# An attention kernel's last two pairs: one store moved to GpSimd's queue, some blocks and copies moved between VectorE and ScalarE

## The chip, the core and the metric

The kernel runs on one core of a Trainium2 chip. The metric is the device time of one execution in microseconds; a profiled execution also gives a span, from its first to its last recorded instruction, and a trace of all instructions and DMA packets.

## What is computed

The reference is linear attention with the feature map relu(x) + 1. For each of 8 x 12 heads, with 512 positions of 64 features (all fp32):

```python
    Q_feat = np.maximum(0, Q) + 1
    K_feat = np.maximum(0, K) + 1
    KV = np.einsum('bhkd,bhkv->bhdv', K_feat, V)
    K_sum = np.sum(K_feat, axis=2)
    numerator = np.einsum('bhqd,bhdv->bhqv', Q_feat, KV)
    denominator = np.einsum('bhqd,bhd->bhq', Q_feat, K_sum)
    return (numerator / (denominator[:, :, :, None] + 1e-10)).astype(np.float32)
```

## The kernel before

The 96 heads are worked on in 12 groups (`g`, 0 to 11) of 8 heads, two groups to a pair (`s`, 0 to 5; NG is 12). Each input of a pair is 2 MB in memory and is loaded by one software DMA from GpSimd's queue, which turns it into bf16 (1 MB in SBUF). The result of a group is 1 MB of fp32.

What each step does, with its line in the profile and its engine:

- `k_features` and `q_features` (L172, VectorE): the feature map, max(x + 1, 1). K's is four instructions of 64x1024 in the pairs 0, 4 and 5 (the list `WIDE`), two of 128x1024 elsewhere; Q's is two of 128x1024 for a group.
- `v_blocks` (L193 on VectorE, L195 on ScalarE): V times each of four 0/1 masks, into `v_all`, so that one product keeps four heads apart. Each of the four masks is one instruction of 128x2048. A cut of 2 gives a mask's whole block to VectorE, a cut of 0 to ScalarE.
- `keys_values` (L219 in the wide pairs, L229 elsewhere, TensorE): K features by V blocks, summed in PSUM (`kva_ps`). It is issued in quarters, with other work in between. `keys_values_copies` (L244) brings the sums to SBUF as bf16 (`kva_all`), in four copies for each pair.
- `transposes` (L257, TensorE) and `transpose_copies` (L262, ScalarE): the Q features turned, through PSUM, into `qt`.
- `out_matmuls` (L275, TensorE) into `o_ps`, and `norms` (L291 and L292, VectorE): the reciprocal of the denominators and the product with the numerators, into `o_sb`. A group has four cells, and `norms` runs once for each.
- `store` (L156 on GpSimd's queue, L161 to L169 on SyncE's): a group's 1 MB to memory. Groups 0 to 9 go by one software DMA each. Group 10 goes by one hardware DMA of SyncE, and group 11 by five smaller ones (512, 256, 61.5, 2.5 and 192 KB).

The order is written out by hand: each engine runs its instructions in the order in which the program issues them. `iteration(s)`, with a = 2s and b = 2s + 1, computes the outputs of the pair before (`output(a - 2)`, `output(a - 1)`) while it makes the key-value sums of its own pair. `output` calls what it is given in `between` after its first and second norms; that is where quarters of `keys_values`, the transposes and, in the last pair alone, the K features of group 11 are put. V blocks for ScalarE are issued at the iteration's top (group b) and before the keys-values copies (the next pair's group a).

Pairs 0 and 1 are started before the loop. Loads are issued two pairs ahead, and the first stores only after iteration 3, behind the last load. So all stores stand in GpSimd's queue behind all loads. After the loop come the outputs of groups 10 and 11 and the stores of both.

Of the kernel before, what the change touches and what calls it, by code (L numbers as in the profile page):

```python
# [19 lines left out]
def kernel(  # L20
# [15 lines left out]
    nc = tc.nc  # L36
# [8 lines left out]
    NP = 4  # L45
    NG = NPAIR // NP
    D1 = D + 1
    W = 2 * D1
    DV = D + 4
# [48 lines left out]
    outs = {}  # L98
# [53 lines left out]
    def store(g):  # L152
        s = g // 2
        o_to = o_dram[:, 2 * NP * s : 2 * NP * s + 2 * NP]
        if g < NG - 2:
            nc.gpsimd.dma_start(  # L156
                out=o_to[:, g % 2 : 2 * NP : 2], in_=outs[s][:, g % 2 : 2 * NP : 2], single_packet=True
            )
            return
        if g == NG - 2:  # L160
            nc.sync.dma_start(out=o_to[:, 0 : 2 * NP : 2], in_=outs[s][:, 0 : 2 * NP : 2])  # L161
            return
        o_sb = outs[s]
        nc.sync.dma_start(out=o_to[:, 1 : 2 * NP : NP], in_=o_sb[:, 1 : 2 * NP : NP])
        nc.sync.dma_start(out=o_to[:, 3], in_=o_sb[:, 3])
        cut = C - 2
        for ps in (slice(0, 123), slice(123, P)):
            nc.sync.dma_start(out=o_to[ps, 7, cut:], in_=o_sb[ps, 7, cut:])
        nc.sync.dma_start(out=o_to[:, 7, 0:cut], in_=o_sb[:, 7, 0:cut])  # L169
# [6 lines left out]
    def k_features(g):  # L176
        k_raw = raw.pop(("k", g))
        kf = kf_of(g)
        for n in range(2):
            if g // 2 in WIDE:  # L180
                for h in range(2):
                    ps = slice(64 * h, 64 * h + 64)
                    feature(kf[ps, :, n, h], k_raw[ps, n])
            else:
                feature(kf[:, :, n], k_raw[:, n])

    def v_blocks(g, engine):
        v_raw = raw["v", g]
        for b in range(4):
            block = v_all[:, g % 2, :, :, b, 0:D]  # L190
            cut = 2 if b < 2 and g < NG - 1 else 0
            if engine == "dve" and cut > 0:
                nc.vector.tensor_scalar_mul(block[:, 0:cut], v_raw[:, 0:cut], mask[:, b : b + 1])  # L193
            if engine == "act" and cut < 2:
                nc.scalar.mul(out=block[:, cut:], in_=v_raw[:, cut:], mul=mask[:, b : b + 1])  # L195

    def q_features(g):
        q_raw = raw.pop(("q", g))
        qf = qf_pool.tile([P, R, C // 4, 2, D, 2], BF16, name="qf")
        for n in range(2):  # L200
            feature(
                qf[:, :, :, n].rearrange("p r c d x -> p r c x d"),
                q_raw[n].rearrange("p r (c x) d -> p r c x d", x=2),
            )
        qfs[g] = qf

    def keys_values(g, lo=0, hi=C2):
        kf = kf_of(g)
        if g % 2 == 0 and lo == 0:
            kva_ps[g // 2] = [psum_kva.tile([P, BANK], FP32, name="kva_ps") for _ in range(2)]  # L210
        halves = kva_ps[g // 2]
        for c in range(lo, hi):
            for n in range(2):
                if g < 2:
                    eight, first, last_c = g, (c, n) == (0, 0), (c, n) == (C2 - 1, 1)
                else:
                    eight, first, last_c = n, g % 2 == 0 and c == 0, g % 2 == 1 and c == C2 - 1
                if g // 2 in WIDE:
                    nc.tensor.matmul(  # L219
                        halves[eight][:, 0 : 4 * DV],  # L220
                        lhsT=kf[:, c, n],
                        rhs=v_all[:, g % 2, n, c],
                        start=first,
                        stop=last_c,
                    )
                    continue
                for h in range(2):
                    ps = slice(64 * h, 64 * h + 64)
                    nc.tensor.matmul(  # L229
                        halves[h][64 * eight : 64 * eight + 64, 0 : 4 * DV],  # L230
                        lhsT=kf[ps, c, n],
                        rhs=v_all[ps, g % 2, n, c],
                        start=first,
                        stop=last_c,
                    )

    def keys_values_copies(s):
        halves = kva_ps[s]
        for h in range(2):
            kva = kva_diag[(2 * s + h) % NV]  # L240
            for n in range(2):
                ps = slice(64 * n, 64 * n + 64)
                tile_, at = (n, slice(64 * h, 64 * h + 64)) if s in WIDE else (h, ps)
                nc.scalar.copy(  # L244
                    out=kva[ps, :, n, :],
                    in_=halves[tile_][at, 0 : 4 * DV].rearrange("p (b x) -> p b x", b=4)[:, :, 0:D1],
                )

    def transposes(g):

        qf = qfs.pop(g).rearrange("p r c n d x -> p r c (n d x)").bitcast(FP32)
        if g % 2 == 0:
            qts[g // 2] = mid_pool.tile([P, C // 2, P, R, 2], BF16, name="qt")
        qt_ps[g] = [psum_qt.tile([P, R, P], FP32, name="qt_ps") for _ in range(2)]
        for half in range(2):
            for r in range(R):
                nc.tensor.transpose(qt_ps[g][half][:, r], qf[:, r, half], identity)  # L257

    def transpose_copies(g):
        to = qts[g // 2].rearrange("p c q r x -> p c (q r x)").bitcast(FP32)  # L260
        for half, t in enumerate(qt_ps.pop(g)):
            nc.scalar.copy(  # L262
                out=to[:, g % 2 * 2 + half].rearrange("p (q r) -> p q r", r=R),
                in_=t.rearrange("p r q -> p q r"),
            )
# [35 lines left out]
    def output(g, between=()):  # L301

        cells = [(g, h, i) for h in range(2) for i in range(2)]
        for k in range(4):
            if k >= 2:
                norms(*cells[k - 2])
                if k - 2 < len(between):
                    between[k - 2]()
            out_matmuls(*cells[k])
        norms(*cells[2])  # L310
        norms(*cells[3])

    def iteration(s):


        a, b = 2 * s, 2 * s + 1
        end = b == NG - 1
        quarter = C2 // 4

        def turned(g):  # L320
            transposes(g)
            transpose_copies(g)

        def first_half():
            turned(a)
            if not end:
                turned(b)
            keys_values(b, 0, quarter)

        def second_half():  # L330
            if end:
                turned(b)
            keys_values(b, quarter, 2 * quarter)

        def second_quarter():
            if end:
                k_features(b)
            keys_values(a, quarter, 2 * quarter)

        v_blocks(b, "act")  # L340
        output(a - 2, (lambda: keys_values(a, 0, quarter), second_quarter))
        keys_values(a, 2 * quarter, C2)
        q_features(a)
        q_features(b)
        if not end:
            k_features(b)
            v_blocks(b, "dve")
        output(a - 1, (first_half, second_half))
        keys_values(b, 2 * quarter, C2)
        if not end:  # L350
            v_blocks(a + 2, "act")
        keys_values_copies(s)
        if not end:
            k_features(a + 2)
            v_blocks(a + 2, "dve")
# [6 lines left out]
    with tc.manual_schedule():  # L362
# [7 lines left out]
        for t in kf_all:  # L370
# [3 lines left out]
            out=mask,  # L374
            in_=identity.rearrange("p (h b x) -> p b h x", h=2, b=4),
# [3 lines left out]
        for i in range(2):  # L379
# [3 lines left out]
                out=t[:, :, :, D], in_=mask[:, None, :].to_broadcast([P, 2 * C2, 4])  # L383
# [14 lines left out]
        keys_values(1)  # L398
        load_pair(2)
        keys_values_copies(0)  # L400
        blocks(2)
        for s in range(1, NG // 2):
            iteration(s)
            if s + 2 < NG // 2:
                load_pair(s + 2)
            for g in range(2 * s - 2, 2 * s) if s > 3 else range(2 * s) if s == 3 else ():
                store(g)
        output(NG - 2)
        output(NG - 1)
        for g in range(NG - 2, NG):  # L410
            store(g)
# [30 lines left out]
```

## Time and profile before

| | |
|---|---|
| Median of 3 runs | 125.42 us (125.40 to 125.49) |
| Profiled execution | 125.89 us, with a span of 124.1 us |
| VectorE busy | 91.3 us (74%) |
| TensorE busy | 77.2 us (62%) |
| ScalarE busy | 72.7 us (59%) |
| GpSimd busy | 26.4 us (21%) |
| DMA, software queue | 28.84 MB, 94.3% of 16 engines' span |
| DMA, hardware queue | 3.15 MB, 7.1% |
| HBM | 37.75 MB read, 12.58 MB written |
| Mean granted TensorE clock | 0.885 |

How to read the profile: times are microseconds from the start of the span. PE is TensorE, PEld its weight loads, DVE VectorE, ACT ScalarE, POOL GpSimd and SP SyncE; a q behind a name is that engine's queue. In a timeline a row is: start, time from its start to its end, engine, line, operation, output<-input with shapes, number of instructions, and in brackets the idle time before it and what ended it. In a table of stretches a row has the busy time of each engine with its count, the granted clock, the mean busy share of the 16 DMA engines and the GB/s that they moved (counted in the bytes written). A DMA lands when its semaphore has been raised; each of the engines that carry it raises it by a part when its own part is through, so that the packet records and the semaphore show when each engine was done.

### The profile page before, as it was taken

The numbers are of one execution on the slowest core, as the hardware profiler recorded it, in microseconds if no ns is written. First come the engines' busy times: TensorE is split into PE (matmuls) and PEld (weight loads), VectorE is DVE, ScalarE is ACT, GpSimd is POOL, SyncE is SP. The second block draws the span as 40 slices with busy tenths as digits, with TensorE's granted clock in tenths as the row PEclk, the third lists the DMA queues.
The fourth block names the chain that finished last, engine by engine and source line by source line (L and its number), as shares of the span: only waits on it lengthen the run. The fifth ranks groups of instructions, "written<-read, shape, count | busy, mean of one in ns | idle before, by whom it ended". The sixth has DMA issues, their size and how long they took to land.

```text
span 124.1 us, 2515 instructions
## 1 busy us (share of the span) xinstructions
PE 77.2 (62%) x1056; PEld 55.4 (45%) x1056; DVE 91.3 (74%) x187; ACT 72.7 (59%) x75; POOL 26.4 (21%) x52
## 2 busy tenths in 40 slices
PE   0000089992398768767699751999497797974500
PEld 0000057771266545645466541567256575762300
DVE  5789772009159999999979989659949999629920
ACT  0005939719982999499964999104943999331000
POOL 6990000600000330006000591210302008020000
PEclk9999999999559999999959996579869999999755
DMA  4999999999999999999999999999999999999993
GB/s 100 323 215 211 213 218 216 211 211 214 217 214 218 215 213 211 218 214 213 215 216 214 213 216 215 216 211 214 214 331 421 421 411 417 417 413 415 392 391 121
DMA packets 8900, 32.15 MB, mean 259 GB/s; under 512 B 568, under 2 KB 824, under 8 KB 8760
## 3 DMA queue, kind: packets, MB, share of 16 engines
q0 software_dynamic: 7520, 28.84, 94.3%
q1 hardware_dynamic: 1368, 3.15, 7.1%
q8 instruction: 8, 0.13, 0.4%
q14 instruction: 4, 0.03, 0.1%
HBM read 37.75 MB, written 12.58 MB: 406 GB/s over the span
## 4 chain that ended last, share of the span: by engine, by line
DVE 36%; PE 25%; DMA 20%; ACT 10%; issue 3%; POOL 1%; ACTq 0%; POOLq 0%
PE kva_ps L219 16%; DVE o_sb L292 13%; DMA k_raw<-in_K_dram 13%; DVE qf L172 7%; DMA v_raw<-in_V_dram 7%; ACT v_all L195 6%; DVE kf_all L172 6%; DVE v_all L193 6%; PE o_ps L275 4%; PE qt_ps L257 3%; DVE recip L291 3%; ACT qt L262 2%; PE kva_ps L229 2%; DVE o_sb L172 1%; ACT L195 1%
## 5 line engine op out<-in xcount | busy, mean ns | idle before, releaser
L195 ACT ACTIVATE v_all<-v_raw,mask 128x2048 bf16<-128x2048 bf16 x26 | 50.4, 1994 | 2.3 <-DMA v_raw<-in_V_dram 2.1
L219 PE MATMUL kva_ps<-v_all,kf_all 128*128 128x272 bf16 x192 | 30.0, 318 | 21.3 <-ACT v_all L195 15.8
L292 DVE TENSOR_TENSOR o_sb<-o_ps,recip 128x512 f32<-128x512 f32 x48 | 33.2, 692 | 1.6
L219 PEld LDWEIGHTS <-kf_all 128*128 128x128 bf16 x192 | 20.2, 109 | 28.1 <-DVE v_all L193 16.0
L275 PE MATMUL o_ps<-kva_all,qt 128*64 128x130 bf16 x384 | 20.2, 241 | 9.0 <-ACT kva_all L244 5.3
L262 ACT COPY qt<-qt_ps 128x512 f32<-128x512 f32 x24 | 12.9, 588 | 17.2 <-PE qt_ps L257 17.0
L275 PEld LDWEIGHTS <-qt 128*64 128x64 bf16 x384 | 13.8, 118 | 18.5 <-issue 9.2
L229 PE MATMUL kva_ps<-v_all,o_sb 64*64 64x272 bf16 x384 | 17.2, 316 | 7.0 <-ACT v_all L195 4.1
L291 DVE RECIPROCAL recip<-o_ps 128x8 f32<-128x8 f32 x48 | 9.7, 201 | 12.3 <-PE o_ps L275 12.3
L193 DVE TENSOR_SCALAR v_all<-v_raw,mask 128x2048 bf16<-128x2048 bf16 x22 | 15.6, 752 | 0.9 <-DMA v_raw<-in_V_dram 0.9
L156 POOL DMA_DIRECT2D out_dram<-o_sb x10 | 9.7, 980 | 29.2 <-DVE o_sb L292 21.9
L229 PEld LDWEIGHTS <-o_sb 64*64 64x64 bf16 x384 | 11.3, 120 | 9.9 <-issue 6.4
L257 PE MATMUL qt_ps<-identity,qf 128*128 128x128 f32 x96 | 13.3, 281 | 3.0 <-DVE qf L172 1.6
L172 DVE TENSOR_SCALAR qf<-q_raw 128x1024 bf16<-128x1024 bf16 x22 | 14.8, 751 | 0.4 <-DMA q_raw<-in_Q_dram 0.4
L129 POOL DMA_DIRECT2D v_raw<-in_V_dram x5 | 3.7, 731 | 54.0 <-ACT qt L262 41.1
L244 ACT CAST kva_all<-kva_ps 64x260 bf16<-64x260 f32 x24 | 8.9, 372 | 9.3 <-PE kva_ps L219 8.9
L172 DVE TENSOR_SCALAR kf_all<-k_raw 64x1024 bf16<-64x1024 bf16 x24 | 11.6, 484 | 1.6 <-DMA k_raw<-in_K_dram 1.3
L257 PEld LDWEIGHTS qt_ps<-identity,qf 128*128 128x128 f32 x96 | 10.2, 140 | 5.4 <-DVE qf L172 2.6
L172 DVE TENSOR_SCALAR o_sb<-k_raw 128x1024 bf16<-128x1024 bf16 x12 | 4.5, 422 | 8.4 <-DMA k_raw<-in_K_dram 8.4
L195 ACT ACT_TABLE_LOAD x1 | 1.3, 1283 | 10.6 <-DMA v_raw<-in_V_dram 10.6
L91 DVE MEMSET kf_all<- 64x1024 f32 x4 | 3.6, 912 | 1.8 <-PEq L426 1.0
L142 POOL DMA_DIRECT2D q_raw<-in_Q_dram x5 | 3.7, 733 | 0.0
(15 smaller groups left out, 14.0 us busy)
## 6 DMA issues: line engine op xcount, KB each, us to landing
out_dram<-o_sb POOLq DMA_DIRECT2D x10, 1024.0 KB, 23.9
v_raw<-in_V_dram POOLq DMA_DIRECT2D x5, 1024.0 KB, 13.0
k_raw<-in_K_dram POOLq DMA_DIRECT2D x5, 1024.0 KB, 17.2
q_raw<-in_Q_dram POOLq DMA_DIRECT2D x5, 1024.0 KB, 21.3
o_sb<-in_Q_dram SPq DMA_DIRECT2D x1, 1024.0 KB, 4.9
k_raw<-in_K_dram POOLq DMA_DIRECT2D x2, 512.0 KB, 9.6
v_raw<-in_V_dram POOLq DMA_DIRECT2D x2, 512.0 KB, 11.5
out_dram<-o_sb SPq DMA_DIRECT2D x1, 1024.0 KB, 5.0
```

What stands on the lines that cost most here:

```text
L156: nc.gpsimd.dma_start(out=o_to[:, g % 2 : 2 * NP : 2], in_=outs[s][:, g % 2 : 2 * NP : 2], single_packet=True)
L172: nc.vector.tensor_scalar(out=dst, in0=src, scalar1=1.0, scalar2=1.0, op0=ALU.add, op1=ALU.max)
L193: nc.vector.tensor_scalar_mul(block[:, 0:cut], v_raw[:, 0:cut], mask[:, b : b + 1])
L195: nc.scalar.mul(out=block[:, cut:], in_=v_raw[:, cut:], mul=mask[:, b : b + 1])
L219: nc.tensor.matmul(halves[eight][:, 0 : 4 * DV], lhsT=kf[:, c, n], rhs=v_all[:, g % 2, n, c], start=first, stop=last_c,)
L229: nc.tensor.matmul(halves[h][64 * eight : 64 * eight + 64, 0 : 4 * DV], lhsT=kf[ps, c, n], rhs=v_all[ps, g % 2, n, c], start=first, stop=l ...
L244: nc.scalar.copy(out=kva[ps, :, n, :], in_=halves[tile_][at, 0 : 4 * DV].rearrange("p (b x) -> p b x", b=4)[:, :, 0:D1],)
L257: nc.tensor.transpose(qt_ps[g][half][:, r], qf[:, r, half], identity)
L262: nc.scalar.copy(out=to[:, g % 2 * 2 + half].rearrange("p (q r) -> p q r", r=R), in_=t.rearrange("p r q -> p q r"),)
L275: nc.tensor.matmul(o_ps[64 * j : 64 * j + 64, c // 2 % 2, (c % 2) * W : (c % 2) * W + W], lhsT=qt[:, c // 2, q : q + 16, :, c % 2], rhs=kv ...
L291: nc.vector.reciprocal(out=recip, in_=cells[:, :, :, :, D:D1])
L292: nc.vector.tensor_tensor(out=outs[g // 2][:, 2 * h + g % 2 : 2 * NP : NP, 4 * i : 4 * i + 4].rearrange("p n (b c) d -> p b c n d", b=2), ...
```

## The change

Three things change, all in the last pairs.

1. The store of group 10 goes by one software DMA from GpSimd's queue, in the form that groups 0 to 9 have, in place of one hardware DMA of SyncE.
2. In pair 4 the odd group (9) gets the order that pair 5's odd group (11) has: ScalarE makes all four of its V blocks, where VectorE made two, and its K features are issued after the second norm of the outputs of group 6 (in `second_quarter`), where they came after the Q features of groups 8 and 9.
3. In the last pair (5) two of the four keys-values copies are made by VectorE, those with h equal to n.

```diff
     def store(g):
...
-        if g < NG - 2:
+        if g < NG - 1:
             nc.gpsimd.dma_start(
                 out=o_to[:, g % 2 : 2 * NP : 2], in_=outs[s][:, g % 2 : 2 * NP : 2], single_packet=True
             )
-            return
-        if g == NG - 2:
-            nc.sync.dma_start(out=o_to[:, 0 : 2 * NP : 2], in_=outs[s][:, 0 : 2 * NP : 2])
             return
...
-            cut = 2 if b < 2 and g < NG - 1 else 0
+            cut = 2 if b < 2 and g not in (NG - 3, NG - 1) else 0
...
-                nc.scalar.copy(
-                    out=kva[ps, :, n, :],
-                    in_=halves[tile_][at, 0 : 4 * DV].rearrange("p (b x) -> p b x", b=4)[:, :, 0:D1],
-                )
+                from_ = halves[tile_][at, 0 : 4 * DV].rearrange("p (b x) -> p b x", b=4)[:, :, 0:D1]
+                if s == NG // 2 - 1 and h == n:
+                    nc.vector.tensor_copy(out=kva[ps, :, n, :], in_=from_)
+                else:
+                    nc.scalar.copy(out=kva[ps, :, n, :], in_=from_)
...
+        late = b >= NG - 3
...
         def second_quarter():
-            if end:
+            if late:
                 k_features(b)
             keys_values(a, quarter, 2 * quarter)
...
-        if not end:
+        if not late:
             k_features(b)
             v_blocks(b, "dve")
```

## The prediction

> **What bounds the kernel now.** I read the page first: is an engine or the DMA full, and until when?
>
> ```profile
> DMA  4999999999999999999999999999999999999993
> ...
> q0 software_dynamic: 7520, 28.84, 94.3%
> q1 hardware_dynamic: 1368, 3.15, 7.1%
> ```
>
> The 16 DMA engines are full from 3 to 121 us; no compute engine is (VectorE 74%). The chain of waits ends in VectorE's norms, but a chain follows one releaser at a time and can't show that the transfers behind it are late anyway. So next the tail: SyncE's issues, and the DMA in half microseconds (last columns: granted clock, DMA share, GB/s).
>
> ```profile
> 115.24 0.39 SPq L161 DMA_DIRECT2D out_dram<-o_sb  x1
> 116.92 0.38 SPq L164 DMA_DIRECT2D out_dram<-o_sb  x1
> ...
> 119.86 0.37 SPq L169 DMA_DIRECT2D out_dram<-o_sb  x1
> ```
> ```profile
> 115.00:115.50 0.50, 0.23 (x8) 0.23 (x8) 0.47 (x3) 0.00 (x0) 0.00 (x0) 1.00 1.02 418
> ...
> 116.00:116.50 0.50, 0.39 (x8) 0.39 (x8) 0.47 (x3) 0.00 (x0) 0.00 (x0) 0.60 0.89 360
> ...
> 118.00:118.50 0.50, 0.00 (x0) 0.00 (x0) 0.50 (x1) 0.00 (x0) 0.00 (x0) 0.50 1.04 406
> ...
> 121.50:122.00 0.50, 0.00 (x0) 0.00 (x0) 0.00 (x0) 0.00 (x0) 0.00 (x0) 0.50 0.81 284
> 122.00:122.50 0.50, 0.00 (x0) 0.00 (x0) 0.00 (x0) 0.00 (x0) 0.00 (x0) 0.50 0.29 99
> 122.50:123.00 0.50, 0.00 (x0) 0.00 (x0) 0.00 (x0) 0.00 (x0) 0.00 (x0) 0.50 0.10 37
> ```
>
> VectorE is done at 118.57, yet the engines still work at full share until 121.5: a backlog of stores. The packet records of the trace split it. Software stores move 4096 bytes in 160 ns per engine, hardware stores 2048 in 84 ns. The engines are not level: group 9's software store ends on the first engine at 115.74, on seven by 116.29, on the last at 117.32. Hardware packets begin at 116.13, on an engine only once its software store is through: until 117.0, 77 have started, and the freed engines alone had room for 81. The last store (L169) lands on 13 engines by 122.66 and on three more at 123.01, 123.05 and 123.20: those that also carry the 123-partition piece of L168 (41 packets of 512 bytes at 27 ns). From 123.20 to the span's end, 124.12, is the closing barrier.
>
> **How far ahead compute gets.** The middle of pair 4, before:
>
> ```profile
> 79.59 0.21 DVE L291 RECIPROCAL recip<-o_ps 128x8 f32<-128x8 f32 x1 [0.99 <-PE o_ps L275]
> ...
> 82.09 0.21 DVE L291 RECIPROCAL recip<-o_ps 128x8 f32<-128x8 f32 x1 [1.57 <-PE o_ps L275]
> ...
> 85.68 1.73 DVE L172 TENSOR_SCALAR kf_all<-k_raw 64x1024 bf16<-64x1024 bf16 x4
> 87.42 1.42 DVE L193 TENSOR_SCALAR v_all<-v_raw,mask 128x2048 bf16<-128x2048 bf16 x2
> ```
> ```profile
> 85.28 1.07 ACT L262 COPY qt<-qt_ps 128x512 f32<-128x512 f32 x2 [7.09 <-PE qt_ps L257]
> ```
> ```profile
> 88.89 1.97 PE L219 MATMUL kva_ps<-v_all,kf_all 128*128 128x272 bf16 x8 [1.83 <-DVE v_all L193]
> ```
>
> *V blocks of group 9 to ScalarE.* Removes two VectorE instructions, 1.42 us, from between the query features and the norms of group 7; adds two at 1.95 to ScalarE, whose four then run from 74.29 to 82.1. ScalarE had nothing from 78.2 to 85.28, so they cost nothing; without that gap, 3.9 us.
>
> *K features of group 9.* The four instructions (1.73) leave 85.68 and come after group 6's second norm, 78.60 to 80.35. K is there (the same load fed group 8 at 72.82). They fill the 0.99 idle and push the third norm by 0.76, inside the 1.57 idle that follows; the fourth still starts at 82.09. Cost nothing; without those gaps 1.73.
>
> So group 7's norms start at 85.7, not 88.75: 3.05 sooner on VectorE. TensorE's keys-values of group 9 follow its transposes at 87.06, not 88.89: 1.83 sooner. They ran at half clock, 1.97 us for the first eight and 1.49 for the next against 1.09 in warm stretches, behind an idle 1.83; breaks of up to 1.13 in the trace cost no clock. With no break I count another 0.88 + 0.40, so 3.1; at the slow clock 1.83. Pair 5's loads don't stop this: store waits on their semaphores show V landed by 83.2 and K by 88.08; Q, behind them, ends when the rate doubles at 91.5 and is read at 99.
>
> *Keys-values copies of the last pair.* Two of four go to VectorE, idle from 109.57 to 111.76. The first two ran one after the other on ScalarE (372 ns mean); side by side TensorE starts 0.38 sooner. VectorE's price has no row of this shape; between its 128x8 reciprocal (0.20) and its 128x512 multiply (0.69) I take 0.4, so zero to 0.4 gained.
>
> Sum: compute ends 3.5 us sooner (1.8 to 3.9), near 115.1.
>
> **What that is worth at the end.** Not 3.5 us, since the backlog doesn't move. Per engine, for the stores from group 9's on:
>
> *Slowest engine.* Software store 9 until 117.32 as before; then group 10's as 16 software packets, 2.51 us (the pitch between stores 8 and 9 there), in place of 32 hardware ones, 2.66; then group 11's: 16 + 8 packets of 2048 and 8 of 1536, 2.54 at the packet times, 2.37 at the pitch that was seen. It ends at 122.2 to 122.4 and lands 0.33 later, 122.5 to 122.7 (before 122.66).
>
> *The three with the extra piece.* Only engines free by about 116.5 fit their end: 56 x 84 + 41 x 27 + 8 x 65 ns is 6.33 us, and their data ended at 122.7 to 122.9. They waited for SyncE: for the first hardware packet, and again before the last pieces, issued at 118.60 to 119.86. With issues 3.5 us sooner and a software store waiting in the ring they don't wait: 115.74 to 116.29, plus 2.51, plus 3.65, plus 0.33, lands at 122.2 to 122.8.
>
> The last landing goes from 123.20 to about 122.6: 0.6 us (0.4 to 0.7). That supposes that the software store is in the ring when the fast engines run out at 115.74. Group 10's last norm would end at 115.21 - 3.5 = 111.7; GpSimd's issue takes 0.75, and the longest lead in the trace, issue to first packet, is 3.6 us (first K load): 115.3 at the worst. GpSimd has nothing queued behind this issue but its closing drain. SyncE loses one issue of 0.39, off the path. The semaphore it reuses belongs to store 2, landed by 100.
>
> Of the 0.6, the kind of store as such is worth 2.66 - 2.51 = 0.15 on the slowest engine: 160 against 168 ns per 4096 bytes. The Trainium skill's page "DMA: Bandwidth & Descriptors", section "Issuing engine by pattern", speaks against that part: simple stores go to SyncE, whose path is generally faster. With the first-byte latencies in its "Specifications" (about 1 us against 0.6) an estimate would take 0.4 off the gain and give 125.2; the trace's full ring has work to do in that time.
>
> **Rivals.**
>
> *The closing drain of GpSimd takes over (slower).* GpSimd ends with a drain that was hidden before:
>
> ```profile
> L437 POOLq DRAIN  x1: 9174/9174/9174, 109.8 to 109.8; - x1
> ```
>
> It waits on no semaphore, and ends at 119.02, 1.27 after store 9's last landing at 117.75: I read that as waiting for software DMAs. After the change the last software landing counts. If software and hardware packets alternate on an engine, group 10's store ends among the last, at about 122.3 + 0.43 landing; the drain ends at 124.0, the barrier takes 0.74 more: 124.7, which is 0.6 worse, 126.0. It decides once the last software landing is past 122.1. For it: the drain's end; a 16 KB code fetch (at 100.26) that broke into the middle of a store. Against: no hardware packet started on an engine with a software store in hand, and in the first microseconds software waited for hardware in the same way, engine by engine. If the software ring goes first, store 10 lands by 120.3 and the drain ends at 121.5, harmless. Chance 0.14.
> The same page, section "Queues, rings and completion order", says each engine takes turns between its queues packet by packet. That rule would give this rival's order; the records at 116 to 117 don't show it.
>
> *Turns by whole stores (no change).* Hardware pieces go in between stores 8, 9 and 10; the slowest engine then has 114.81 + 1.34 + 2.51 + 0.67 + 2.51 = 121.8 for store 10, landing 122.2, drain 123.5, end 124.2: 125.5. The records can't tell this from "ring first", since only one software store was left. Chance 0.12.
>
> *Compute gains little.* Under about 1.3 us (TensorE's clock stays low and GpSimd's issues slow VectorE more), fast engines run dry as before, and the last piece goes out at about 119: 125.2 to 125.7. Chance 0.08, half of it no change, half slower.
>
> *The norms, not the queue, set the end.* Then 3.5 us come off: 121.9. The queue doesn't allow it: 12.58 MB of stores behind the last load (91.5) at 418 GB/s end at 121.6 even on level engines, which with 0.33 and 0.92 is a span of 122.85 and a time of 124.15. Chance 0.01, for what lies between that and the forecast.
>
> **Numbers.** Forecast, chance 0.65: -0.6 against the profiled execution (125.89 with its span of 124.12) is 125.3; the median of the runs is 125.42, and I take the same 0.6 off it: 124.8, its own range 124.5 to 125.1. The 8-in-10 range takes in the turns by whole stores and half the third rival, and below most of a levelling of the engines that I don't count: 124.3 to 125.7. About 0.2% (0.25 us) is what a measurement of this kernel can tell from no change. Faster: 0.65 + 0.01 = 0.66. Same: 0.12 + 0.04 = 0.16. Slower: 0.14 + 0.04 = 0.18.
>
> **What would show it.** Right: group 7's first norm near 85.7; keys-values of group 9 at 1.1 us for eight; last norm ending at 114.7 to 116.8; DMA share at 1.0 without the dip to 0.89 at 116; store 10 landing near 120.3, the last store near 122.6; GpSimd's drain done before SyncE's last wait. Wrong: the drain ending last, a gap in the DMA before store 10, or last norms later than 117.

## The result, and the profile after

The changed kernel is slower: 125.99 us against 125.44 on the same chip, a ratio of 1.0042 (95% interval 1.0027 to 1.0057), 0.55 us. Two later comparisons gave 126.01 (1.0036, 1.0011 to 1.0061) and 125.95 (1.0040, 1.0012 to 1.0068). The forecast was 124.8.

The page of the changed kernel shows the megabyte that moved from the hardware queue to the software queue, and DMA engines as full as before:

```profile
DMA  3999999999999999999999999999999999999992
...
q0 software_dynamic: 7792, 29.89, 96.5%
q1 hardware_dynamic: 840, 2.10, 4.5%
```

Compute did what the prediction said. Two rows of VectorE's timeline before, group 7's first norm and the last norm:

```profile
88.75 0.20 DVE L291 RECIPROCAL recip<-o_ps 128x8 f32<-128x8 f32 x1
...
117.88 0.69 DVE L292 TENSOR_TENSOR o_sb<-o_ps,recip 128x512 f32<-128x512 f32 x1
```

These are rows of VectorE's, TensorE's and ScalarE's timelines after; lines have moved (L289 and L290 are the norms, L216 the keys-values of the wide pairs, L192 ScalarE's V blocks, L243 VectorE's new copies):

```profile
82.20 0.21 DVE L289 RECIPROCAL recip<-o_ps 128x8 f32<-128x8 f32 x1 [0.88 <-PE o_ps L273]
...
85.56 0.21 DVE L289 RECIPROCAL recip<-o_ps 128x8 f32<-128x8 f32 x1
...
107.55 0.92 DVE L243 CAST kva_all<-kva_ps 64x260 bf16<-64x260 f32 x2 [1.00 <-PE kva_ps L216]
...
114.61 0.69 DVE L290 TENSOR_TENSOR o_sb<-o_ps,recip 128x512 f32<-128x512 f32 x1
```
```profile
87.32 1.09 PE L216 MATMUL kva_ps<-v_all,kf_all 128*128 128x272 bf16 x8
```
```profile
74.92 7.68 ACT L192 ACTIVATE v_all<-v_raw,mask 128x2048 bf16<-128x2048 bf16 x4
```

Group 6's fourth norm is where it was (82.20, before 82.09). Group 7's first comes at 85.56 and not at 88.75. The keys-values of group 9 run at the full clock, 1.09 us for eight. The last norm ends at 115.3 and not at 118.6.

The tail is where it went wrong. First SyncE's issues (start, length) after the change:

```profile
113.65 0.39 SPq L161 DMA_DIRECT2D out_dram<-o_sb  x1
115.33 0.34 SPq L162 DMA_DIRECT2D out_dram<-o_sb  x1
115.71 2.42 SPq L165 DMA_DIRECT2D out_dram<-o_sb  x2
118.17 1.01 SPq L166 DMA_DIRECT2D out_dram<-o_sb  x1
```

Group 11's issues begin 3.3 us sooner than before (113.65, before 116.92), but the last three take 1.0 to 1.2 us each, where such issues took about 0.4. The first hardware packet of group 11 moves at 116.37, 2.7 us after its issue; before, group 10's hardware store had its first packet 0.9 after its issue. Next the DMA in half microseconds after the change (last two columns: DMA share, GB/s):

```profile
115.50:116.00 0.50, 0.00 (x0) 0.00 (x0) 0.00 (x0) 0.00 (x0) 0.00 (x0) 0.50 0.98 401
116.00:116.50 0.50, 0.00 (x0) 0.00 (x0) 0.00 (x0) 0.00 (x0) 0.00 (x0) 0.50 1.03 422
116.50:117.00 0.50, 0.00 (x0) 0.00 (x0) 0.00 (x0) 0.00 (x0) 0.00 (x0) 0.50 1.01 414
...
121.50:122.00 0.50, 0.00 (x0) 0.00 (x0) 0.00 (x0) 0.00 (x0) 0.00 (x0) 0.50 0.76 283
122.00:122.50 0.50, 0.00 (x0) 0.00 (x0) 0.00 (x0) 0.00 (x0) 0.00 (x0) 0.50 0.22 78
122.50:123.00 0.50, 0.00 (x0) 0.00 (x0) 0.00 (x0) 0.00 (x0) 0.00 (x0) 0.50 0.01 3
```

The dip at 116 is gone, as forecast, and the queue is through a little sooner than in the first trace of before: the last landing is 122.98, against 123.20. Yet the span is 124.19, against 124.12. The closing instructions of GpSimd (POOLq) and SyncE (SPq) between 122.4 and 123.5, after, with count, length in ns, and start:

```profile
L436 SPq DRAIN  x2: 7/7/7, 123.1 to 123.1; - x2
L436 POOLq DRAIN  x1: 11189/11189/11189, 112.2 to 112.2; - x1
L436 POOLq EVENT_SEMAPHORE  x1: 17/17/17, 123.5 to 123.5; - x1
```

SyncE has waited for all stores by 123.12, the start of its second drain; below, that is when SyncE is "ready". GpSimd's drain, begun at 112.22, ends at 123.41, and only then does GpSimd take its step of the barrier. Before, that drain was over at 119.02. Group 10's software store landed on its last engine at 122.10, and the drain ended 1.31 later. A drain that ends before SyncE is ready is called hidden below.

### The profile page after: what moved, and what is told of

It is laid out like the page before. It is cut to its first block, busy times and chain, and to the rows that moved or that the text cites. A ratio compares the mean times of both kernels' runs of the same rounds, so it can differ in the third digit from the quotient of the medians.

```text
span 124.2 us, 2518 instructions
## 1 busy us (share of the span) xinstructions
PE 75.9 (61%) x1056; PEld 54.9 (44%) x1056; DVE 89.9 (72%) x187; ACT 75.8 (61%) x75; POOL 28.7 (23%) x53
## 4 chain that ended last, share of the span: by engine, by line
DVE 46%; PE 27%; ACT 9%; DMA 7%; issue 2%; POOL 1%; DVEq 0%; ACTq 0%; POOLq 0%
DVE o_sb L290 18%; PE kva_ps L216 17%; DVE qf L169 8%; DVE v_all L190 8%; DMA v_raw<-in_V_dram 7%; ACT v_all L192 6%; DVE kf_all L169 5%; PE o_ps L273 4%; DVE recip L289 4%; PE qt_ps L255 4%; DVE o_sb L169 3%; PE kva_ps L226 3%; ACT L192 1%; ACT qt L260 1%; DVE kva_all L243 1%
## 5 line engine op out<-in xcount | busy, mean ns | idle before, releaser
L192 ACT ACTIVATE v_all<-v_raw,mask 128x2048 bf16<-128x2048 bf16 x28 | 54.2, 1994 | 2.3 <-DMA v_raw<-in_V_dram 2.1
L216 PE MATMUL kva_ps<-v_all,kf_all 128*128 128x272 bf16 x192 | 29.3, 313 | 19.6 <-ACT v_all L192 16.4
L290 DVE TENSOR_TENSOR o_sb<-o_ps,recip 128x512 f32<-128x512 f32 x48 | 33.2, 691 | 1.6
L216 PEld LDWEIGHTS <-kf_all 128*128 128x128 bf16 x192 | 20.1, 108 | 25.8 <-DVE v_all L190 16.1
L273 PE MATMUL o_ps<-kva_all,qt 128*64 128x130 bf16 x384 | 19.5, 236 | 9.1 <-ACT kva_all L245 4.7
L273 PEld LDWEIGHTS <-qt 128*64 128x64 bf16 x384 | 13.3, 116 | 18.5 <-issue 7.5
L156 POOL DMA_DIRECT2D out_dram<-o_sb x11 | 12.0, 1102 | 28.7 <-DVE o_sb L290 15.0
L289 DVE RECIPROCAL recip<-o_ps 128x8 f32<-128x8 f32 x48 | 9.6, 200 | 8.7 <-PE o_ps L273 8.6
L190 DVE TENSOR_SCALAR v_all<-v_raw,mask 128x2048 bf16<-128x2048 bf16 x20 | 14.3, 756 | 1.4 <-DMA v_raw<-in_V_dram 1.4
L169 DVE TENSOR_SCALAR kf_all<-k_raw 64x1024 bf16<-64x1024 bf16 x24 | 11.0, 459 | 1.8 <-DMA k_raw<-in_K_dram 1.5
L245 ACT CAST kva_all<-kva_ps 64x260 bf16<-64x260 f32 x22 | 8.2, 372 | 5.9 <-PE kva_ps L216 5.4
```

What stands on the lines that cost most here:

```text
L156: nc.gpsimd.dma_start(out=o_to[:, g % 2 : 2 * NP : 2], in_=outs[s][:, g % 2 : 2 * NP : 2], single_packet=True)
L169: nc.vector.tensor_scalar(out=dst, in0=src, scalar1=1.0, scalar2=1.0, op0=ALU.add, op1=ALU.max)
L216: nc.tensor.matmul(halves[eight][:, 0 : 4 * DV], lhsT=kf[:, c, n], rhs=v_all[:, g % 2, n, c], start=first, stop=last_c,)
L245: nc.scalar.copy(out=kva[ps, :, n, :], in_=from_)
L273: nc.tensor.matmul(o_ps[64 * j : 64 * j + 64, c // 2 % 2, (c % 2) * W : (c % 2) * W + W], lhsT=qt[:, c // 2, q : q + 16, :, c % 2], rhs=kv ...
L289: nc.vector.reciprocal(out=recip, in_=cells[:, :, :, :, D:D1])
```

## The experiments

Two theories were open from the start: the drain behind a late software store (D), and a tail made longer by mixing both kinds of packets (Q), with the reordered compute as a third (C). Every edit below starts from the kernel before or from the changed kernel, as said.

**e1, the software store alone** (kernel before):

```diff
-        if g < NG - 2:
+        if g < NG - 1:
...
-        if g == NG - 2:
-            nc.sync.dma_start(out=o_to[:, 0 : 2 * NP : 2], in_=outs[s][:, 0 : 2 * NP : 2])
-            return
```

> Part 1 alone: group 10's store goes by GpSimd's software queue, compute is as before. Before: 125.42 us; changed kernel 125.99. Theory D (the closing drain of GpSimd waits for the last software landing and holds the closing barrier): the drain ends about 1.3 us after store 10's last landing; since group 11's hardware pieces are issued only at 117 to 120, store 10 is ahead of most of them and lands near 121, drain near 122.3, hidden: 125.2 to 125.6. Rival Q (hardware and software packets on one engine hinder each other, and that makes the tail longer, whatever the drain does): 125.6 to 126.0. Rival C (the cost comes from the compute reordering): no change, 125.4.

Measured 125.31 against 125.41, ratio 0.9997 (0.9973 to 1.0021). The software store landed at 120.93, the drain ended at 122.24, and SyncE's last wait was over at 122.76: hidden, as D says. Rival Q asked for 125.6 or more; the median speaks against it, though the interval reaches 125.67.

**e2, the compute order alone** (changed kernel with the stores of before, its L155 to L162):

```diff
-        if g < NG - 1:
+        if g < NG - 2:
...
+        if g == NG - 2:
+            nc.sync.dma_start(out=o_to[:, 0 : 2 * NP : 2], in_=outs[s][:, 0 : 2 * NP : 2])
+            return
```

> Parts 2 and 3 alone: the compute order of the changed kernel, with group 10's store left on SyncE. Last norm ends near 115.3, as in the changed kernel. Theory D: the last software store is group 9's, landing by 119 or so, so the drain is hidden and the end is SyncE's last wait: 124.9 to 125.3, faster than before. Rival Q: group 10's and 11's hardware packets meet two software stores in the ring, SyncE's issues stall (over 1 us each in place of 0.4) and the tail is no shorter: 125.4 to 125.8. Rival C: 126.0, as the changed kernel.

Measured 125.35 against 125.41, ratio 0.9989 (0.9971 to 1.0008). Rival C is out. So is the gain that D's expectation still held: the norms end at 114.76, and it buys nothing measurable. In that Q came as near as D: SyncE's last three issues took 1.0 to 1.2 us, as Q had said, and the tail was no shorter. Neither half of the change costs anything that can be measured; only the two together do.

**e3, the drain by itself** (kernel before, the last hardware piece made a software one):

```diff
-        nc.sync.dma_start(out=o_to[:, 7, 0:cut], in_=o_sb[:, 7, 0:cut])
+        nc.gpsimd.dma_start(out=o_to[:, 7, 0:cut], in_=o_sb[:, 7, 0:cut])
```

> The kernel before, with only the last piece (group 11's 192 KB) issued by GpSimd in place of SyncE, so that a software DMA is the last to land. Theory D: the drain ends 1.3 us after that landing and the barrier 0.75 later, in place of 0.9 after the landing: about 1.1 us more, 126.3 to 126.8, by a drain whose end in the trace is the last software landing + 1.3. Rivals Q and C, with a drain that waits for nothing of the sort: 125.3 to 125.8 (a software issue in place of a hardware one).

Measured 126.48 against 125.41, ratio 1.0073 (1.0048 to 1.0099): 1.07 us for the same bytes, issued at the same place in the program. Its closing rows between 122.4 and 123.5:

```profile
L437 SPq DRAIN  x2: 7/7/7, 123.3 to 123.4; - x2
L437 POOLq DRAIN  x1: 6922/6922/6922, 117.2 to 117.2; - x1
```

The software piece landed at 122.79. SyncE was ready at 123.36; the drain, begun at 117.19, ended at 124.11, 1.32 after the landing, and the span 0.78 after that.

**e4, the kernel before once more**, unchanged:

> The kernel before once more, unchanged, for a second trace: how far the last landing, the spread of the 16 engines within a store (1.6 us for group 9 in the first trace) and the time vary from one execution to the next. The first profiled execution took 125.89 us against a median of 125.42, so all theories expect a last landing nearer 122.8 than 123.2, and 125.3 to 125.6.

The median was 125.41, as in the other runs of the kernel before beside it. The expectation of a calmer profiled execution missed: this one took 126.91. Its last norm ended at 119.58, SyncE's last piece went out at 120.86, and three engines landed it at 124.17 to 124.22, the other thirteen by 123.05. So executions with one order of compute differ in when it ends by several microseconds (118.6 and 119.6 in the two traces of the kernel before, 116.0 to 119.6 in the five with the old order), and a late one waits for SyncE in the tail.

**e5, the hardware pieces later** (changed kernel, the pieces of the last rows first):

```diff
+        cut = C - 2
+        for ps in (slice(0, 123), slice(123, P)):
+            nc.sync.dma_start(out=o_to[ps, 7, cut:], in_=o_sb[ps, 7, cut:])
         nc.sync.dma_start(out=o_to[:, 1 : 2 * NP : NP], in_=o_sb[:, 1 : 2 * NP : NP])
         nc.sync.dma_start(out=o_to[:, 3], in_=o_sb[:, 3])
-        cut = C - 2
-        for ps in (slice(0, 123), slice(123, P)):
-            nc.sync.dma_start(out=o_to[ps, 7, cut:], in_=o_sb[ps, 7, cut:])
```

> The changed kernel, with group 11's five hardware pieces issued in another order: the two small pieces of its last rows first, which must wait for the last norm, so that SyncE issues nothing before about 115.3 (113.65 before that). Theory D (GpSimd's drain ends 1.3 us after the last software landing and holds the barrier; hardware packets that arrive while group 10's software store is in the ring take turns with it and push its landing to 122.1): the hardware pieces come about 1.7 us later, store 10 lands by 120.5 to 121.6, the drain is over by 123.0, and the time falls to 125.3 to 125.7. Rival S (the 0.55 us lies in the spread of the engines or in the sooner compute, not in the drain): 125.9 to 126.2, as the changed kernel.

Measured 125.34 against 125.38, ratio 0.9997 (0.9986 to 1.0008): the loss is gone, with the same instructions on every compute engine and the same store of group 10. The software store landed at 120.31, the drain ended at 121.63, SyncE was ready at 122.76.

**e6, group 10 on ScalarE's hardware queue** (changed kernel):

```diff
-        if g < NG - 1:
+        if g < NG - 2:
...
+        if g == NG - 2:
+            nc.scalar.dma_start(out=o_to[:, 0 : 2 * NP : 2], in_=outs[s][:, 0 : 2 * NP : 2])
+            return
```

> The changed kernel, with group 10's store issued from ScalarE's hardware queue in place of GpSimd's software queue (ScalarE is done near 108). Theory D: the last software landing is group 9's, near 118 to 119, the drain is hidden, the end is SyncE's last wait: 125.2 to 125.5, like the compute order alone (125.35). Rival S: 125.9 to 126.2.

Measured 125.35 against 125.38, ratio 0.9994 (0.9985 to 1.0004). The drain ended at 121.29, hidden. Group 9's store, the last software one, landed at 120.02 and not near 118 to 119.

**e8 and e9, what sooner norms are worth with a shorter queue.** Both leave out the store of group 0; e8 from e2's kernel, e9 from the kernel before:

```diff
     def store(g):
+        if g == 0:
+            return
```

> The compute order of the changed kernel with group 10's store on SyncE, and without the store of group 0 (its 1 MB of the output is not written). If the queue of stores sets the end (theory Q), 1 MB less is 2.5 us less: 122.7 to 123.3 against 125.35 with it. If the end is set by when the norms are done and the last piece goes out (theory N), little changes: 124.8 to 125.3.

> The kernel before without the store of group 0 (its 1 MB of the output is not written). Its last norm ends at 116.0 to 119.6 in the traces so far (compute order as before), the last piece goes out 1.3 later and lands about 2.1 to 3.3 after that. With the queue 2.5 us shorter the norms set the end here: 123.3 to 124.6, so that the compute order, worth nothing with the full queue, is worth 0.5 to 1.5 us against the same kernel with the new order. If compute order is worth nothing in itself, both are the same, 122.9.

Measured 122.88 and 124.46, against 125.38 for the kernel before. With the new order all of the megabyte's 2.5 us comes off, and four executions lie within 0.05 us. With the old order 0.9 comes off at the median, and the executions scatter from 122.84 to 125.68 (one more, at 182.74, stands outside). By its five fastest executions (median 124.28) its ratio to the kernel before is 0.9874 (0.9839 to 0.9909), against 0.9793 (0.9780 to 0.9806) with the new order. So sooner norms are worth 1.0 us by these ratios and 1.4 by these medians, within the 0.5 to 1.5 expected, as soon as the queue is not in their way; with the full queue they are worth nothing measurable.

**e7, half the software store** (changed kernel; the rows that are ready first by software, the others by SyncE):

```diff
+        if g == NG - 2:
+            nc.gpsimd.dma_start(out=o_to[:, 0 : 2 * NP : NP], in_=outs[s][:, 0 : 2 * NP : NP], single_packet=True)
+            nc.sync.dma_start(out=o_to[:, 2 : 2 * NP : NP], in_=outs[s][:, 2 : 2 * NP : NP])
+            return
```

> The changed kernel with group 10's store in two halves of 512 KB: the half that is ready after its second norm by software DMA (some 1.7 us sooner and half as long), the other by SyncE. Theory D: the last software landing is 119.5 to 121.2, the drain ends before 122.5, hidden: 125.2 to 125.5. Rival S: 125.8 to 126.1.

Measured 125.44 against 125.46, ratio 0.9995 (0.9971 to 1.0018). Its software half landed later than expected, at 121.59, with engines spread by 2.5 us; the drain ended at 122.90, still before SyncE's 123.56.

**e10 and e13, the changed kernel again.** Both its first traces had the engines wider apart within a store than most others: 2.07 and 2.08 us for group 8's, against 1.4 to 1.8 in most. That spread is a rival of its own (S).

> The changed kernel once more, for a second trace. Theory D: whatever the execution's compute does, the drain of GpSimd ends 1.27 to 1.32 us after the last software landing and later than SyncE's last wait, and the span ends 0.75 after the drain: last software landing 121.7 to 122.4, 125.8 to 126.1. Rival S (the first trace's 2 us spread of the engines within a store made it slow): with a spread of 1.4 to 1.6 it is no slower than 125.5.

> The changed kernel for a third trace, on the chip of the two variants above. In its traces so far the drain of GpSimd ended 0.29 and 0.05 us after SyncE's last wait, and the engines were spread by 2.1 us. Theory D: the drain ends last again, and the more so the smaller the spread. Rival S: with a spread under 1.8 the kernel takes 125.5 or less.

In e10 the software store landed at 122.02 and the execution took 125.88, both as D had it, but the spread was 2.08 again, so that S was not put to the test. The drain ended at 123.33, 0.05 after SyncE was ready: with such a spread SyncE's own landing (123.14) is nearly as late, and the drain alone explains little of that execution. e13 decides. Its spread is 1.56, and its last hardware landing, 122.69, is within 0.1 us of those in e1 and e5 (122.62 in both), whose traced executions took 125.30. Its closing rows between 122.4 and 123.5:

```profile
L436 SPq DRAIN  x2: 7/7/7, 122.8 to 122.8; - x2
L436 POOLq DRAIN  x1: 12345/12345/12345, 111.2 to 111.2; - x1
```

SyncE was ready at 122.83; the drain, begun at 111.17, ended at 123.51, 0.68 later and 1.31 after the software landing at 122.20. The execution took 126.06. S would have it at 125.5 or less. Q, a longer tail whatever the drain does, would have SyncE ready later than in e1 and e5 (122.76) by the whole loss; it was 0.07 later.

**e14, the late pieces again**, beside e13 on one chip:

> The changed kernel with group 11's pieces of the last rows first, once more, beside the changed kernel on the same chip. Theory D: drain over before SyncE's last wait, 125.3 to 125.5, 0.5 to 0.7 us less than the changed kernel here, whatever the spread. Rival S: no difference between the two on one chip.

Measured 125.48, where the changed kernel took 125.95 (0.47 more, just under the 0.5 that D expected) and the kernel before 125.51; ratio to before 0.9988 (0.9969 to 1.0007). Software landing 120.36, spread 1.56 as in e13. Its closing rows over the whole span (three drains each; GpSimd's long one and SyncE's first two are those of the tail):

```profile
L436 POOLq DRAIN  x3: 51/93/11282, 110.4 to 123.1; - x3
...
L436 SPq DRAIN  x3: 7/7/7, 122.6 to 122.9; - x3
```

GpSimd's long drain starts at 110.4 and is over 11.28 later, at 121.7; SyncE is ready at 122.65.

**e11 and e12, the start of the hardware packets moved a little** (changed kernel). e11 exchanges the first two pieces; e12 cuts the first one in two:

```diff
-        nc.sync.dma_start(out=o_to[:, 1 : 2 * NP : NP], in_=o_sb[:, 1 : 2 * NP : NP])
         nc.sync.dma_start(out=o_to[:, 3], in_=o_sb[:, 3])
+        nc.sync.dma_start(out=o_to[:, 1 : 2 * NP : NP], in_=o_sb[:, 1 : 2 * NP : NP])
```
```diff
-        nc.sync.dma_start(out=o_to[:, 1 : 2 * NP : NP], in_=o_sb[:, 1 : 2 * NP : NP])
+        for i in range(2):
+            cs = slice(4 * i, 4 * i + 4)
+            nc.sync.dma_start(out=o_to[:, 1 : 2 * NP : NP, cs], in_=o_sb[:, 1 : 2 * NP : NP, cs])
```

> The changed kernel with the first two of group 11's hardware pieces in the other order, so that SyncE issues nothing before the sixth of the last eight norms (about 115.3) but all other pieces in their order: a start of the hardware packets between the changed kernel's (issue at 113.65) and the order with the last rows first. Theory D with turns by packet: fewer hardware packets get in ahead of the end of store 10, which lands at 120.5 to 121.5; the drain is hidden or nearly so: 125.3 to 125.7. Rival S (the spread of the engines, which comes from earlier in the kernel): 125.9 to 126.1.

> The changed kernel with group 11's first piece cut in two, so that half of it is issued 0.84 us sooner, after the first of its norms. Theory D with turns by packet: hardware packets get in sooner, the software store lands as late as before or later (122.0 to 122.6), the drain ends the kernel: 126.0 to 126.5. Rival S: 125.9 to 126.1. (Packets of 1 KB in place of 2 KB may add 0.1.)

e11: 125.61 against 125.51, ratio 1.0002 (0.9981 to 1.0024); software landing 121.02, drain over at 122.33, hidden. e12: 125.57, ratio 1.0000 (0.9976 to 1.0024), where 126.0 or more was expected. Its software store landed sooner (121.71) and the drain tied with SyncE (123.03 and 123.04). The reason is in the packet records. On an engine that serves nothing else the store's 16 packets take 2.51 us (e5, e14). In e13, on ten of the 16 engines (told apart by the order in which they finish), they take 3.77 or 3.78: 1.27 more, which is 15 hardware packets of 84 ns, one between each two software packets. In e12 the first hardware packets are 1 KB, and the store takes 3.17 on 14 engines: 0.66 more, 44 ns for each of 15 turns (such a packet takes 46). The engines take turns packet by packet, so small hardware packets delay the software store less. The expectation had the start of the packets in it, but not that a turn of half the bytes is half as long.

Over these sixteen traces, the two of the first comparison among them, two lines hold: GpSimd's long drain ends 1.23 to 1.32 us after the last software landing, and the span ends 0.77 to 0.78 after the later of that drain and SyncE's last wait. The time of an execution is 1.77 to 1.81 us more than its span in all of them.

No version beat the kernel before by more than the measurements can tell: e1, e2, e5, e6, e7 and e14 lie between 0.9988 and 0.9997 of it, each with 1 in its interval.

## Why the prediction was wrong

**Compute: right.** 3.5 us sooner was the sum, 3.3 came between the first two traces. Over all traces the new order ends its norms at 113.5 to 115.9 (mean of 11: 114.7), the old at 116.0 to 119.6 (mean of 5: 117.6): 2.9 sooner. V blocks and K features cost nothing where they were put; group 9's keys-values ran at the full clock without the break; VectorE's copies took 0.42 and 0.43 where 0.4 was taken.

**The order on the engines: the step that failed.** The prediction said that the software ring goes first, so that store 10 lands by 120.3 and the drain is harmless. It read this from the kernel before, where no hardware packet started on an engine with a software store in hand. That window could not show it: the hardware store was issued at 115.24, and the last engine was free of software at 117.32, 2.1 us later. With more software in the ring the first hardware packet came 1.9 to 4.2 us after its issue, and where a software store was then still under way the two took turns. That the late start is what hid the turns from that window fits these figures; what delays the start was not tested. Store 10 landed at 122.0 to 122.2 in the three traces of the changed kernel, 1.7 to 1.9 us later than predicted. On e13's last engine, the one that finishes last each time, the landings give the whole difference: 115.30 for store 8, 118.44 for store 9 (3.14 later, where 2.51 is the time without turns), 122.20 for store 10 (3.76 later); 0.63 and 1.25 are the turns, and without them it would be 120.3.

So the first rival's mechanism, which had a chance of 0.14, is what happened: the drain was last. That its 126.0 came so near to 125.99 is in part luck. It had the drain end at 124.0, and measured were 123.3 to 123.5. The prediction also turned the rival's span of 124.7 into a time by adding 1.3 (the median less the profiled span), where every trace has 1.77 or more between its own time and span: 124.7 would have been 126.5. The second rival's moments were the nearer ones, with store 10 landed at 122.2, the drain over at 123.5 and the end at 124.2 (measured 124.1 to 124.3), but its cause was not: the turns go by packet, not by whole stores. By the same step from span to time the prediction called 124.2 no change (125.5); the traces make it 126.0. The point from which the drain decides, a software landing past 122.1, fits the first trace of before (SyncE ready at 123.34); against SyncE's 122.83 in e13 it is some 121.5.

The rule that the prediction set against its row, in the Trainium skill's page "DMA: Bandwidth & Descriptors", section "Queues, rings and completion order", is that an engine goes round its queues a packet at a time. The traces bear it out: 1.27 us of 84 ns turns in e13, 0.66 of half-size turns in e12.

**The gain at the end: the term that was mis-sized.** The forecast took 0.6 us off for fast engines that no longer wait for SyncE, and took it off the median as well. e2, e6 and e14 have the sooner compute and no exposed drain, and their medians are 0.03 to 0.06 us below the kernel before, which no interval tells from nothing. The forecast's span, 124.12 less 0.6, is 123.5; e1 and e5 reached it (123.53 in both), and those executions took 125.30, not 124.8. The 0.6 belonged to the profiled execution, which stood 0.47 above the median and had its norms at 118.58. e4 shows the same thing more strongly (norms at 119.58, 126.91 us), and e1, with the old order but norms at 116.0, took 125.30. That the median execution has little of that wait fits these three; it was not traced for an execution at the median of the kernel before. The rest of the step held: the queue is the floor, and e8 shows it, since one megabyte less takes 2.47 us off e2's time.

**The kind of store: no measurable part.** 0.15 us was expected from software packets; e1's interval is too wide to see it.

## What to carry to other kernels

When stores fill the queue to the end, as here, sooner compute is worth nothing measurable by itself, and it matters which kind of transfer lands last: a late software store can cost a microsecond that an equal hardware store doesn't (1.07 us in e3), through what follows it at the kernel's end. Before a term is taken off, ask whether the profiled execution is a median one; a wait that exists only in a late execution isn't there to be saved, and a span of one execution is not turned into a time by the median of others. And a row that shows one queue waiting for another shows it only for as long as the row lasts.

## What the runs showed of the hardware

GpSimd's closing drain follows the last software DMA by 1.23 to 1.32 us in all sixteen traces, while SyncE goes on 0.14 us after a hardware landing (122.69 to 122.83 in e13). A hardware store issued well before the software stores run out starts late: its first packet came 1.9 to 4.2 us after its issue in thirteen traces, against 0.9 in three (the two of the kernel before, and e9), where the first engines were through with software by the issue or within 0.5 us of it. Most of SyncE's later issues then take 0.8 to 1.6 us in place of 0.4. Where both kinds are in hand on an engine they take turns packet by packet (3.77 us in place of 2.51 for 16 software packets in e13, 3.17 in e12). The 16 engines of one core finish the same store 1.4 to 2.5 us apart, differently in each execution, and the gap often opens near 98 us; what opens it was not tested.
